# Starting every operand of TensorE at one SBUF byte address modulo 512

## The chip, the core and the metric

The kernel is one program on one core of a Trainium2 chip. The metric is device time of one execution in microseconds (us). Before the change the median of three runs is 1791.74 us (1791.64 to 1792.22). The core has five engines that matter here: TensorE (PE in the rows: matmuls, with PEld for the loads of the stationary operand), VectorE (DVE), ScalarE (ACT), GpSimd (POOL) and SyncE (SP, which issues most transfers). SBUF is the on-chip memory: 128 partitions, and every tile takes the same byte range in each of them. PSUM holds matmul results.

A matmul has two operands in SBUF. The *stationary* one (up to 128 columns) is loaded into the array first, which the rows show as LDWEIGHTS on PEld; the *moving* one (up to 512 columns) is then streamed through it. In a row `ps<-hx,wh 128*128 128x512` the moving tile is `hx`, the stationary one `wh`; 128*128 are rows and columns of the stationary operand, 128x512 is the result.

## The reference

Two layers of a diffusion transformer over 256 tokens and 256 context tokens, width 2048, branch width 4096, all in float32. Cut to what matters:

```python
# layer 0 (x and ctx alike): h = rmsnorm(x) * (1 + scale) + shift
u, z = split(h @ w_in, 2)                                # 2048 -> 2 x 4096
f = real(fft2(u grouped in 16 x 256, over tokens and channels))
y = (f @ w_mix, group by group) * silu(z)                # 16 matrices 256 x 256
x = x + gate * (y @ w_out[0])                            # 4096 -> 2048
# layer 1 (x only; the context gives keys and values)
q, k, v, z = split(h @ w_in1)
o = attention(rope(q), rope(k), v, window 128, all context keys, a sink per head)
x = x + gate * ((o * silu(z)) @ w_out[1]);  return rmsnorm(x, final_g)
# scale, shift, gate = silu(c) @ ada_w + ada_b, once per layer and per stream
```

## The kernel before, in words

**Precision.** Each float32 operand is split into a high part in the fp32r type (ACT copies it, rounding) and a low part (DVE subtracts): names end in `h` and `l`. `mm3` (lines 78 to 81) multiplies with three fp32r matmuls: high by high (line 79), high by low (line 80), low by high (line 81). Nearly all of PE's work is such triples; lines 1142 and 1144 are a two-matmul form of the same, with results of 512 and 256 columns.

**Stages**, by time in the profile:

- 0 to 51 us: norms, the Fourier transform over tokens as a matmul (`xs` stationary, `dh`/`dl` moving, 256 columns) and transposes.
- 51 to 144 us, first z: six blocks of z for layer 0 (`ext` tiles moving, 512 columns, `wh`/`wl` stationary), mixed with float32 matmuls for scale and shift (line 320).
- 144 to 378 us, **u stage**: 16 groups. For each, weights of u are loaded, folded into a difference `m` and a sum `p` of 127 columns for each of 16 row blocks (`load_uh`, `split_uh`), and split into `wmh`, `wml`, `wph`, `wpl`. `part` multiplies them as stationary operands with `hx` and `act` tiles moving: 256 columns for `m`, 260 for `p`. `load_m` prepares the mixing matrix of the group (`mh`/`ml` moving, tables `ch`/`cl` stationary), and `mix` multiplies that (`pqh`, `pql`, `sp` stationary) with the split results (`am`, `aph`/`apl`, `asp` moving).
- 378 to 670 us, rest of z: 26 blocks of 48 matmuls, weights `wh`/`wl` stationary, activations moving, 512 columns; of the 16 row blocks' activation tiles some lie in pool `hx`, some in pool `act` (`h_tile`).
- 670 to 1021 us, first output projection: 32 times 48 matmuls, 512 columns; moving are `hx` tiles.
- 1031 to 1116 us, keys and values of layer 1: moving are the weights `wh`/`wl`, stationary the activations `h1` (pool `h1`) and `h1c`.
- 1116 to 1640 us, q, z and attention, in an order written out by hand.
- 1640 to 1779 us, last projection: weights moving, stationary the split results `yh[k]` in 32 tiles from several pools; those for k from 28 on lie in the pool `fin` and are named `ys`, as are the 12 before them, which lie in `h1`.

**Where a tile lies** is set by the pools: a pool takes a range of bytes in each partition, a tile its offset in it, and sizes of the tiles that stand before it shift all that follow. Tiles of 2048 or 4096 bytes in a row keep the same address modulo 512; a small tile ahead of them moves them all.

**What sets the order of the work.** The framework's scheduler orders each engine's instructions by a timing model of its own, from the program's dependencies; only the attention part is written out (`tc.manual_schedule`). So a change of an instruction's shape can reorder the stages around it. Each engine then works through its list in order, with semaphore waits. A tile buffer that is used again makes the next writer wait for the last reader. Big weights come over SP's queue into `raw` (3 buffers of 8 KB per partition), split halves go into `ws` (6 buffers of 4 KB), the split weights of u into `wf` (8 of 4 KB).

The addresses of the operands, in bytes modulo 512, read from the built programs:

| operand tiles | where they are used | before | after |
|---|---|---|---|
| `wh`, `wl` in `ws`; `act`; `raw` | all over | 192 | 256 |
| `hx` | moving in u, rest of z, first projection | 256 | 256 |
| `ext` | moving in first z | 352 | 256 |
| `wmh`, `wml`, `wph`, `wpl`, row block k of 8 | stationary in u | 256 - 4k | 256 |
| `mh`, `ml` of `load_m` | moving | 480 | 256 |
| `ch`, `cl`; `pqh`, `pql`, `sp`; `asp` | u stage | 256 | 256 |
| `am` (named `mh`, `ml` too) | moving in `mix` | 288 | 256 |
| `aph`, `apl` (1040 bytes each) | moving in `mix` | 352, 384, 416, 448 | the same |
| `dh`, `dl`, `xs` | first stage | 256 | 256 |
| `h1`, `h1c`, `ye`, `ys` in `h1`, `kkh`, `kkl`, `qa`, `qb` | layer 1 | 192 | 256 |
| `ys` in `fin` (k from 28) | stationary, last projection | 256 | 256 |
| `raw2` (line 320, float32) | moving in first z | 448 | 448 |

Of the kernel before, what the change touches and what calls it, by code (L numbers as in the profile page):

```python
# [10 lines left out]
F32 = mybir.dt.float32  # L11
F32R = mybir.dt.float32r
# [4 lines left out]
P = 128  # L17
# [5 lines left out]
G = 16  # L23
# [6 lines left out]
def tile_dit(ctx: ExitStack, tc: tile.TileContext, a: dict, out: bass.AP):  # L30
# [24 lines left out]
    def cload(name, shape, q=None, pool=const):  # L55
        t = pool.tile(shape, F32, tag=name, name=name)
        (q or nc.gpsimd).dma_start(t, a[name])
        return t
# [73 lines left out]
    def wf(name, dt=F32):  # L132
        return wfp.tile([P, 1024], dt, tag="wf", name=name)

    def split_uh(v, m, nms=("m", "p")):
        fl = {}
        for nm, t in [(nm, {"m": m, "p": v}[nm]) for nm in nms]:
            l, h = (wf(f"w{nm}{x}", F32R)[:, : 8 * 127].rearrange("p (k c) -> p k c", k=8) for x in "lh")
            split(h, l, t)
            fl[nm] = (h, l)  # L140
        return fl
# [15 lines left out]
    adap = lay0.enter_context(tc.tile_pool(name="ada", bufs=1))  # L157
# [22 lines left out]
    with tc.tile_pool(name="st", reuse_waits="tile", bufs=1, side="right") as st, ExitStack() as sts:  # L180
        dm = sx.tile([P, 2, N], F32, name="dm")
        ss = st.tile([P, 4, 4], F32, name="ss")
        rr = st.tile([P, 4], F32, name="rr")
        f0 = st.tile([P, KT, 2], F32, name="f0")
        sh16 = st.tile([P, KT, 2], F32, name="sh16")

        cnt = [0]

# [298 lines left out]
        for i in range(4):  # L487
            for j in range(4):
                k = 4 * i + j
# [28 lines left out]
        for b in range(NE):  # L518
            z = ext()
# [1 line left out]
            nc.gpsimd.dma_start(zd[b], z)  # L521

    uc = us.enter_context(tc.tile_pool(name="uc", reuse_waits="tile", bufs=2, side="right"))
    mk = cload("mk", [96, G], pool=adap)
    wsr = wsp.tile([P, 512], F32, tag="ws", name="wsr")
    nc.gpsimd.dma_start(wsr, a["wsp"])
    sphl = []
# [7 lines left out]
    def load_m(g):  # L535
        m = uc.tile([P, 2, GD], F32, tag="m", name="m", bufs=1) if g else wsp.tile([P, 2, GD], F32, tag="ws", name="m")
        (nc.scalar if g else nc.gpsimd).dma_start(m, a["wm"][g])
        mt = wsp.tile([P, 2, GD], F32, tag="ws", name="mt")
        lr = uc.tile([P, 2, GD], F32R, tag="ml", name="ml")
        mh = uc.tile([P, 2, GD], F32R, tag="mh", name="mh")  # L540
        V.tensor_tensor(mt[:, 0], m[:, 0], m[:, 1], op=ALU.add)
        V.tensor_tensor(mt[:, 1], m[:, 0], m[:, 1], op=ALU.subtract)
        split(mh, lr, mt)
        o = psum()
        mm3(o[:, 0:GD], ch[:, 0, :], cl[:, 0, :], mh[:, 0, :], lr[:, 0, :], True, False)
        PE.matmul(o[:, 0:GD], ch[:, 2, :], mh[:, 1, :], start=False, stop=False)
        PE.matmul(o[:, 0:GD], ch[:, 2, :], lr[:, 1, :], start=False, stop=True)
        mm3(o[:, GD : 2 * GD], ch[:, 1, :], cl[:, 1, :], mh[:, 1, :], lr[:, 1, :], True, True)
        o2 = psum()
        PE.matmul(o2[0:96, 0:GD], ch[:, 3, 0:96], mh[:, 0, :], start=True, stop=False)  # L550
        PE.matmul(o2[0:96, 0:GD], ch[:, 3, 0:96], lr[:, 0, :], start=False, stop=True)
        pqh = ua.tile([P, 512], F32R, tag="pqh", name="pqh")
        pql = ua.tile([P, 512], F32R, tag="pql", name="pql")
        split(pqh, pql, o)
        sp = ua.tile([96, GD], F32R, tag="sp", name="sp")
        S.activation(sp, o2[0:96, 0:GD], AF.Copy, scale=mk[:, g : g + 1])
        V.scalar_tensor_tensor(sp[64:96, :], o2[64:96, 0:GD], mk[64:96, g : g + 1], sp[64:96, :].bitcast(F32), op0=ALU.mult, op1=ALU.subtract)
        return pqh, pql, sp
# [3 lines left out]
    fd = [dram.tile([P, 512], F32, name=f"fd{b}") for b in range(NB)]  # L562
    rawu = us.enter_context(tc.tile_pool(name="rawu", reuse_waits="tile", bufs=1))
    up = us.enter_context(tc.tile_pool(name="up", reuse_waits="tile", bufs=2))
    asp = up.tile([96, 2, 130], F32R, name="asp", bufs=1)
    for g in range(G):
        w = load_u(g) if g else wu0
        if g == 0:
            am = []
            for i in range(2):  # L570
                mh = up.tile([P, 2, P], F32R, name=f"mh{i}", bufs=1)
                ml = up.tile([P, 2, P], F32R, name=f"ml{i}", bufs=1)
                for z in (mh, ml):
                    for s in range(2):
                        S.activation(z[:, s], ident, AF.Copy, scale=0.0)
                am.append((mh, ml))
        if g:
            pqh, pql, sp = load_m(g)
        oa = {}

        def part(xs, ks=range(KT)):
            for nm, c0, c1 in xs:
                if nm not in oa:
                    oa[nm] = psum()[0:127, 0 : 2 * (c1 - c0)].rearrange("p (s j) -> p s j", s=2)
            for k in ks:
                for nm, c0, c1 in xs:
                    wh, wl = w[k // 8][nm]
                    h, l = hx[k]
                    mm3(oa[nm], wh[:, k % 8, :], wl[:, k % 8, :], h[:, :, c0:c1], l[:, :, c0:c1], k == 0, k == KT - 1)

        if g < G - 1:
            part(parts[:1])
        else:
            mix()
            part(parts)
        if g == 0:
            o2 = psum()[0:64, 0:260].rearrange("p (s j) -> p s j", s=2)
            for k in range(KT):
                for x_ in hx[k]:
                    sp_end = PE.matmul(o2, sphl[k // 8][:, k % 8], x_[:, :, 0:130], start=k == 0 and x_ is hx[k][0], stop=k == KT - 1 and x_ is hx[k][1]).ins  # L600
            osl = up.tile([32, 2, 130], F32, name="osl", bufs=1)
            S.copy(osl, o2[32:64])
            osp = up.tile([32, 2, 130], F32, name="osp", bufs=1)
            V.tensor_tensor(osp, o2[0:32], osl, op=ALU.add)
            S.copy(asp[0:32], osp)
            S.copy(asp[64:96], osp)
            V.tensor_tensor(asp[32:64], osp, asp[0:32].bitcast(F32), op=ALU.subtract)
            with tc.issue_after(sp_end):
                pqh, pql, sp = load_m(0)
        mh, ml = am[g % 2]  # L610
        split(mh[0:127, :, 1:128], ml[0:127, :, 1:128], oa["m"][:, :, 1:128])
        if g < G - 1:
            if g:
                mix()
            part(parts[1:])
        ph = up.tile([127, 2, 130], F32R, tag="aph", name="aph")
        pl = up.tile([127, 2, 130], F32R, tag="apl", name="apl")
        split(ph, pl, oa["p"])

        def mix(g=g, mh=mh, ml=ml, ph=ph, pl=pl, pqh=pqh, pql=pql, sp=sp):  # L620
            for db in range(2):
                q = slice(db * P, (db + 1) * P)
                q2 = slice(GD + db * P, GD + (db + 1) * P)
                gs_ = psum()
                gv = gs_[:, 0:256].rearrange("p (s j) -> p s j", s=2)
                mm3(gv, pqh[0:127, q2], pql[0:127, q2], mh[0:127], ml[0:127], True, True)
                gc = psum()
                gcv = gc[:, 0:260].rearrange("p (s j) -> p s j", s=2)
                PE.matmul(gcv, sp[:, q], asp, start=True, stop=False)  # L629
                mm3(gcv, pqh[0:127, q], pql[0:127, q], ph, pl, False, True)  # L630
                gsb = up.tile([P, 2, P], F32, tag="gsb", name="gsb")
                S.copy(gsb, gv)
                ft = up.tile([P, 2, N], F32, tag="ft", name="ft")
                V.tensor_tensor(ft[:, :, 0:128], gcv[:, :, 0:128], gsb, op=ALU.subtract)
                V.tensor_tensor(ft[:, :, 129:256], gcv[:, :, 1:128], gsb[:, :, 1:128], op=ALU.add)
                S.copy(ft[:, :, 128:129], gcv[:, :, 128:129])
                (nc.gpsimd if g < G - 1 else nc.scalar).dma_start(fd[g * 2 + db], ft.rearrange("p s j -> p (s j)"))

        if g == G - 1:
            mix()  # L640
# [38 lines left out]
    with tc.tile_pool(name="yp", reuse_waits="tile", bufs=32) as ypool:  # L679
# [19 lines left out]
        with tc.tile_pool(name="zp", reuse_waits="tile", bufs=2) as zp:  # L699
# [11 lines left out]
            for kg in range(4):  # L711
                wr = rawp.tile([P, D], F32, tag="raw", name="raw")
                last_dma[0] = nc.sync.dma_start(wr.rearrange("p (b c) -> p b c", b=4), a["wz"][NE - 4 : NE, :, kg * 512 : (kg + 1) * 512].rearrange("b p c -> p b c")).ins
                w = []
# [5 lines left out]
                for j in range(4):  # L720
                    k = kg * 4 + j
# [9 lines left out]
            for b in range(NE):  # L731
                z = zp.tile([P, 512], F32, tag="z", name="z")
# [3 lines left out]
            for b in range(NE + 4, NB):  # L736
                w = ws_split(raw(a["wz"][b - 4]))
# [43 lines left out]
        for i in range(32):  # L781
# [3 lines left out]
            w = ws_split(raw(a["wo0"][sw, kg]))  # L785
# [16 lines left out]
            edge = kg in (0, 15)  # L802
# [84 lines left out]
    with tc.tile_pool(name="h1", reuse_waits="tile", bufs=16) as h1p:  # L887
        hx1 = []
        kT = []
        with tc.tile_pool(name="kvp", reuse_waits="tile", bufs=2) as kvp:  # L890
# [18 lines left out]
            for kg in range(8):  # L909
                w = [(kv_h, kv_l)] if kg == 0 else ws_split(raw(a["wkv"][kg]))  # L910
                for j in range(2):
                    k = kg * 2 + j
# [4 lines left out]
                    for tb in range(4):  # L917
                        h = (hx1, hc1)[tb // 2][k]
                        c = (tb % 2) * P
# [27 lines left out]
        with tc.tile_pool(name="ye", reuse_waits="tile", bufs=6) as yep, ExitStack() as ats:  # L947
# [349 lines left out]
            with tc.tile_pool(name="fin", reuse_waits="tile", bufs=1) as fp:  # L1297
# [7 lines left out]
                        nc.gpsimd.dma_start(x2[tb][c], x1d[tb, :, c * 512 : (c + 1) * 512])  # L1305
                fg = fp.tile([P, D], F32, name="fg")
                nc.gpsimd.dma_start(fg, a["fg"].broadcast_to([P, D]))
                ss = fp.tile([P, 10], F32, name="ss")

                def evac(tb, cb, o):  # L1310
                    q, t, x = slice(cb * 512, (cb + 1) * 512), act(), x2[tb][cb]
# [20 lines left out]
                for k in range(28, NB, 2):  # L1332
                    w = w1_next()
# [5 lines left out]
                for kg in range(16):  # L1339
                    w = ws_split(raw(a["wo1b"][kg]))  # L1340
# [179 lines left out]
```

## Time and profile before

| what | value |
|---|---|
| median of three runs | 1791.74 us (1791.64 to 1792.22) |
| span of the profiled execution | 1790.8 us, 27995 instructions |
| what lies around the span, median less span | 0.9 us |
| PE busy | 1770.2 us (99%), 10941 matmuls |
| DVE, ACT, POOL busy | 1376.3 (77%), 880.1 (49%), 185.7 us (10%) |
| moved by DMA | 370.20 MB, mean 207 GB/s |
| granted TensorE clock | full in all 40 slices |

How to read it: the execution's own time is its span and what lies around it, and the page gives the span. A matmul's bar in the rows is longer than the distance to the next one's start, since matmuls are pipelined and their ends are modelled: bars of 0.39 us start every 0.23 us. What sets the time of a stream of matmuls is that distance, which this document calls the *pace*. It can be had from a window of W us that n bars touch: a bar touches it if it starts in the window or up to one bar's length ahead of it, so the pace is (W + bar) / n.

### The profile page before, as it was taken

To read this page: it belongs to the slowest core of one execution; us is meant where nothing else is said; L and a number is where in the kernel's file an instruction comes from. 1 tells how busy PE (TensorE), PEld (TensorE's weight loads), DVE (VectorE), ACT (ScalarE), POOL (GpSimd) and SP (SyncE) were. 2 spreads that over 40 slices of the span, in tenths; PEclk is the share of its full clock that TensorE was granted. 3 is DMA by queue.
4 is the path that set the end of the run, shared out by engine and by line. 5 is a ranking of instruction groups with operands and counts; after the bars stand their busy time and mean duration, and the time that the engine had idled before them with its cause. 6 is when DMAs were issued, how large, how long until landed. Compare 5 with 4: busy or idle time off the path is not lost.

```text
span 1790.8 us, 27995 instructions
## 1 busy us (share of the span) xinstructions
PE 1770.2 (99%) x10941; PEld 1482.2 (83%) x10941; DVE 1376.3 (77%) x2314; ACT 880.1 (49%) x1530; POOL 185.7 (10%) x225
## 2 busy tenths in 40 slices
PE   8999999999999999999999999999999999999997
PEld 6669999987888888888888888888888888887886
DVE  5769999978887887687986473797889888977454
ACT  6545444543222232233332352687678777866343
POOL 0001000020000010000000001133123303301010
PEclk9999999999999999999999999999999999999999
DMA  9994555476766677654566233544444344446553
GB/s 388 420 368 167 200 205 207 165 270 226 306 243 234 255 261 273 266 197 159 211 237 233 104 148 107 187 143 152 152 148 148 139 146 156 143 156 246 195 186 120
DMA packets 69028, 370.20 MB, mean 207 GB/s; under 512 B 8736, under 2 KB 10928, under 8 KB 35360
## 3 DMA queue, kind: packets, MB, share of 16 engines
q1 hardware_dynamic: 55344, 328.51, 49.0%
q0 software_dynamic: 9520, 32.96, 5.4%
q10 hardware_dynamic: 4032, 6.95, 1.1%
q8 instruction: 86, 1.41, 0.3%
q14 instruction: 46, 0.38, 0.1%
HBM read 353.16 MB, written 15.21 MB: 206 GB/s over the span
## 4 chain that ended last, share of the span: by engine, by line
PE 97%; DVE 1%; ACT 1%; issue 0%; DMA 0%; SPq 0%; DVEq 0%
PE ps L79 26%; PE ps L81 25%; PE ps L80 25%; PE ps L1142 7%; PE ps L1219 3%; PE ps L1144 3%; PE ps L320 2%; PE ps L1173 2%; PE ps L1174 2%; PE ps L1015 0%; DMA xn<-in_x 0%; PE ps L600 0%; PE ps L629 0%; PE ps L336 0%; DVE wl L1092 0%
## 5 line engine op out<-in xcount | busy, mean ns | idle before, releaser
L69 ACT CAST wh<-raw 128x1024 fp32r<-128x1024 f32 x178 | 186.8, 1052 | 415.5 <-PE ps L80 369.8
L70 DVE TENSOR_TENSOR wl<-raw,wh 128x1024 fp32r<-128x1024 f32 x178 | 219.9, 1236 | 145.8 <-ACT wh L69 145.3
L79 PE MATMUL ps<-hx,wh 128*128 128x512 f32 x700 | 274.5, 395 | 0.0
L81 PE MATMUL ps<-hx,wl 128*128 128x512 f32 x700 | 273.2, 393 | 0.0
L80 PE MATMUL ps<-hx,wh 128*128 128x512 f32 x700 | 273.0, 390 | 0.0
L1092 DVE TENSOR_TENSOR wl<-raw,wh 128x1024 fp32r<-128x1024 f32 x142 | 190.5, 1347 | 56.6 <-ACT wh L1086 55.8
L1086 ACT CAST wh<-raw 128x1024 fp32r<-128x1024 f32 x142 | 148.8, 1048 | 76.3 <-PE ps L80 55.2
L1142 PE MATMUL ps<-h,wh 128*128 128x512 f32 x512 | 184.3, 399 | 0.0
L666 DVE CUSTOM_DVE_ANT_0 raw<-raw,cb 128x1024 f32<-128x1024 f32 x128 | 154.9, 1220 | 31.8 <-DMA raw<-in_adw 31.1
L81 PEld LDWEIGHTS ps<-hx,wl 128*128 128x128 f32 x700 | 131.4, 188 | 31.0
L80 PEld LDWEIGHTS ps<-hx,wh 128*128 128x128 f32 x700 | 131.4, 188 | 29.6
L79 PEld LDWEIGHTS ps<-hx,wh 128*128 128x128 f32 x700 | 131.5, 188 | 27.8 <-ACT hx L405 0.8
L1144 PE MATMUL ps<-h,wl 128*128 128x256 f32 x512 | 138.6, 281 | 0.0
L666 DVE CUSTOM_DVE_ANT_0 junk<-raw,cb 128x1024 f32<-128x1024 f32 x96 | 117.2, 1221 | 24.8 <-DMA raw<-in_adw 15.0
L79 PE MATMUL ps<-wh,h 128*128 128x512 f32 x320 | 124.8, 396 | 0.2 <-ACT h L899 0.2
L80 PE MATMUL ps<-wl,h 128*128 128x512 f32 x320 | 124.5, 389 | 0.0
L81 PE MATMUL ps<-wh,h 128*128 128x512 f32 x320 | 124.4, 390 | 0.0
L1142 PEld LDWEIGHTS ps<-h,wh 128*128 128x128 f32 x512 | 96.3, 188 | 21.5
L1191 ACT ACTIVATE p<-ps,mx 128x512 f32<-128x512 f32 x128 | 86.8, 683 | 53.4 <-DVE mx L1182 52.9
L1144 PEld LDWEIGHTS ps<-h,wl 128*128 128x128 f32 x512 | 96.6, 189 | 2.9
L81 PE MATMUL ps<-act,wl 128*128 128x512 f32 x234 | 91.0, 394 | 0.7 <-DVE wl L70 0.7
L1182 DVE CUSTOM_DVE_ANT_0 ps<-ps,mask,nsink 128x512 f32<-128x512 f32 x128 | 91.1, 752 | 0.5
(367 smaller groups left out, 4012.8 us busy)
## 6 DMA issues: line engine op xcount, KB each, us to landing
raw<-in_adw SPq DMA_DIRECT2D x64, 1024.0 KB, 4.9
raw<-in_wz SPq DMA_DIRECT2D x58, 1024.0 KB, 4.8
raw<-in_awp SPq DMA_DIRECT2D x32, 1024.0 KB, 12.0
raw<-in_wo SPq DMA_DIRECT2D x32, 1024.0 KB, 4.9
raw<-in_wq SPq DMA_DIRECT2D x32, 1024.0 KB, 4.8
raw<-in_wu SPq DMA_DIRECT2D x25, 1016.0 KB, 5.1
raw<-in_wo1b SPq DMA_DIRECT2D x16, 1024.0 KB, 4.8
act<-in_xT POOLq DMA_DIRECT2D x32, 256.0 KB, 5.6
```

The source lines that it names most:

```text
L69: cast[0] = S.copy(h, t[:, i * 1024 : (i + 1) * 1024]).ins
L70: V.tensor_tensor(l, t[:, i * 1024 : (i + 1) * 1024], h.bitcast(F32), op=ALU.subtract)
L79: PE.matmul(o, wh, xh, start=start, stop=False)
L80: PE.matmul(o, wh, xl, start=False, stop=False)
L81: return PE.matmul(o, wl, xh, start=False, stop=stop).ins
L666: V.tensor_tensor_reduce(junk if s == 0 and i < 3 else wf, wf, cb[:, s], 1.0, 0.0, ALU.mult, ALU.add, acc[:, i, kh, fg * 2 + f, s : s + 1])
L1086: cast[0] = S.copy(h, t[:, i * 1024 : (i + 1) * 1024]).ins
L1092: V.tensor_tensor(ready[n][1], ready[n][2], ready[n][0].bitcast(F32), op=ALU.subtract)
L1142: PE.matmul(o[0], wh[:, q], hx1[k], start=k == 0, stop=k == KT - 1)
L1144: PE.matmul(o[0][:, 0:N], wl[:, q], hx1[k][:, 0:N], start=False, stop=False)
L1182: V.tensor_tensor_reduce(so[tb], so[tb], mask[:, tb, :], -0.125, nsink[:, i : i + 1], ALU.add, ALU.min, mx[:, tb : tb + 1])
L1191: S.activation(pt[:, tb, :], so[tb], AF.Exp, bias=mx[:, tb : tb + 1], scale=-1.0, accum_out=sm[:, tb : tb + 1])
```

## The change

Five edits, all of them on addresses:

- The split weights of u are held at 128 columns for each row block (512 bytes) where they were at 127 (508 bytes); the 127 columns that are used stay the same. The copies and subtractions that write them get the shape 128x8x127 where they had 128x1016.
- Padding tiles: 24 columns `edge` in pool `st`, ahead of `raw3` and `ext` in the right-hand stack; 56 columns `edge` in pool `uc`; the tile `ss` of the last stage grows from 10 to 128 columns.
- The table `mk` (96x16) moves from pool `ada` to pool `const`, which moves `raw`, `ws`, `act` and the pools of layer 1 by 64 bytes.
- The four zero-padded tiles `am` are allocated ahead of `asp`. What is computed, and with how many instructions, stays the same.

```diff
@@ split_uh
-            l, h = (wf(f"w{nm}{x}", F32R)[:, : 8 * 127].rearrange("p (k c) -> p k c", k=8) for x in "lh")
+            l, h = (wf(f"w{nm}{x}", F32R).rearrange("p (k c) -> p k c", k=8)[:, :, 0:127] for x in "lh")
@@ pool st
         sh16 = st.tile([P, KT, 2], F32, name="sh16")
+        st.tile([P, 24], F32, name="edge")
@@ after the first z
-    mk = cload("mk", [96, G], pool=adap)
+    mk = cload("mk", [96, G])
@@ load_m
         mh = uc.tile([P, 2, GD], F32R, tag="mh", name="mh")
+        if g == 1:
+            uc.tile([P, 56], F32, name="edge", bufs=1)
@@ u stage
+    am = [tuple(up.tile([P, 2, P], F32R, name=f"m{x}{i}", bufs=1) for x in "hl") for i in range(2)]
     asp = up.tile([96, 2, 130], F32R, name="asp", bufs=1)
...
-            am = []
-            for i in range(2):
-                mh = up.tile([P, 2, P], F32R, name=f"mh{i}", bufs=1)
-                ml = up.tile([P, 2, P], F32R, name=f"ml{i}", bufs=1)
-                for z in (mh, ml):
+            for pair in am:
+                for z in pair:
                     for s in range(2):
                         S.activation(z[:, s], ident, AF.Copy, scale=0.0)
-                am.append((mh, ml))
@@ last stage
-                ss = fp.tile([P, 10], F32, name="ss")
+                ss = fp.tile([P, P], F32, name="ss")
```

The scheduler answers the new shape with another order in the u stage, and there alone but for one pair swapped on DVE, ACT and PE in the last stage. Lists of SP and POOL are as before. Two places matter to the prediction.

The first is PE in the third group of the u stage: `wph`/`wpl` and `wmh`/`wml` are products with the weights of u, `apl,pqh` and `aph,pql` the second half of `mix` for the group before. Before:

```order
L79 MATMUL ps<-act,wph 127x260
L80 MATMUL ps<-act,wph 127x260
L80 MATMUL ps<-apl,pqh 128x260
L81 MATMUL ps<-aph,pql 128x260
L80 MATMUL ps<-apl,pqh 128x260
L81 MATMUL ps<-aph,pql 128x260
L81 MATMUL ps<-act,wpl 127x260
L79 MATMUL ps<-hx,wph 127x260
```

With the change:

```order
L79 MATMUL ps<-hx,wph 127x260
L80 MATMUL ps<-apl,pqh 128x260
L81 MATMUL ps<-aph,pql 128x260
L80 MATMUL ps<-apl,pqh 128x260
L81 MATMUL ps<-aph,pql 128x260
L80 MATMUL ps<-hx,wph 127x260
L81 MATMUL ps<-hx,wpl 127x260
```

The four products of `mix` stand 16 places into the group's `p` products, where they stood 8 places in.

The second is DVE at the start of the u stage, where the first weights of u and the first mixing matrices are split (`wpl`, `wml`: low parts of the weights; `wm`: a new difference; `ml`, `mt`: the mixing matrix; line 694: activations for the next stage). Before:

```order
L62 TENSOR_TENSOR wml<-wm,wmh 128x1016
L694 SCALAR_TENSOR_TENSOR act<-act,gs_83,r_bc 128x256 x2
L62 TENSOR_TENSOR ml<-mt,mh 128x512
L541 TENSOR_TENSOR mt<-m 128x256
L542 TENSOR_TENSOR mt<-m 128x256
L128 TENSOR_TENSOR wm<-raw 128x1016
L62 TENSOR_TENSOR wpl<-raw,wph 128x1016
L62 TENSOR_TENSOR ml_1643<-ps,mh_1642 127x2x127
L604 TENSOR_TENSOR osp<-ps,osl 32x260
```

With the change:

```order
L62 TENSOR_TENSOR wml<-wm,wmh 128x8x127
L62 TENSOR_TENSOR ml<-mt,mh 128x512
L62 TENSOR_TENSOR wpl<-raw,wph 128x8x127
L62 TENSOR_TENSOR ml_1643<-ps,mh_1642 127x2x127
L694 SCALAR_TENSOR_TENSOR act<-act,gs_83,r_bc 128x256
L604 TENSOR_TENSOR osp<-ps,osl 32x260
L694 SCALAR_TENSOR_TENSOR act<-act,gs_83,r_bc 128x256
L544 TENSOR_TENSOR mt<-m 128x256
L545 TENSOR_TENSOR mt<-m 128x256
L128 TENSOR_TENSOR wm<-raw 128x1016
```

The low part `wpl` of the first group comes ahead of the next group's difference `wm` and mixing matrix `mt`, where it came behind them (lines from 184 on have moved by one to three).

## The prediction

> **What bounds the kernel now.** I read the engines' shares and the chain of work that ended last first, then PE's waits, since a change of addresses can only matter where PE itself sets the time.
>
> ```profile
> PE 1770.2 (99%) x10941; PEld 1482.2 (83%) x10941; DVE 1376.3 (77%) x2314; ACT 880.1 (49%) x1530; POOL 185.7 (10%) x225
> ...
> PE 97%; DVE 1%; ACT 1%; issue 0%; DMA 0%; SPq 0%; DVEq 0%
> ```
>
> ```profile
> PE ps L294 <- DMA xn<-in_x: 5.8, 1, 5.8
> PE ps L79 <- ACT dh L259: 1.7, 1, 1.7
> PE ps L81 <- DVE wl L70: 0.7, 1, 0.7
> PE ps L861 <- ACT act L822: 0.4, 1, 0.4
> PE ps L79 <- ACT h L899: 0.2, 1, 0.2
> ```
>
> PE is 97% of the chain and waits 8.8 us in all, 7.5 of them before its first real stage. So the time is the number of matmuls times their pace, and the question is whether the pace depends on addresses. Windows inside stages that run matmuls of 512 columns only answer it (us, busy and count, clock, DMA share, GB/s):
>
> ```profile
> 440.00:660.00 220.00, 220.00 (x950) 1.00 0.68 256
> 680.00:1010.00 330.00, 330.00 (x1444) 1.00 0.57 213
> 1034.00:1112.00 78.00, 78.00 (x346) 1.00 0.29 109
> 1666.00:1724.00 58.00, 58.00 (x258) 1.00 0.54 196
> ```
>
> With 0.39 us for a bar, the paces are 220.39/950 = 232.0 ns in the rest of z, 330.39/1444 = 228.8 in the first projection, 78.39/346 = 226.6 for keys and values and 58.39/258 = 226.3 in the last projection. PE is busy for every microsecond and the clock is full in all four, so the difference is no wait and no throttle. It is the same mm3 at the same shapes. By the table of addresses the last two windows have both operands at 192 modulo 512. The first projection has the moving one at 256 and the stationary one at 192; the rest of z has the moving one alternately at 192 and 256 over weights at 192.
>
> The cleanest comparison lies inside the last projection, one line and one loop, where only the pool of the stationary tile changes: `fin` tiles at 256, everything else at 192.
>
> ```profile
> 1724.12 0.39 PE L81 MATMUL ps<-wh,act 128*128 128x512 f32 x1
> 1724.34 1.10 PE L79 MATMUL ps<-wh,ys 128*128 128x512 f32 x4
> ...
> 1735.54 0.62 PE L79 MATMUL ps<-wh,ye 128*128 128x512 f32 x2
> ```
>
> ```profile
> 1720.00:1745.00 25.00, 11.36 (x48) 1.00 0.51 184
> ```
>
> The second fence counts the matmuls with `ys` alone: 48 from 1724.34 to 1735.54, which is 233.3 ns each, against 226.3 on either side. A different residue of the two operands costs 2 to 7 ns of 227. I take 226.6 as the pace at equal residues.
>
> **Term 1: 512 columns in z and the projections.** No instruction is added or removed; SP's and POOL's lists stay as they are. After the change all these operands start at 256.
>
> - Rest of z: 26 blocks of 48, 1248 matmuls. At the window's pace, 232.0 less 226.6 on all of them gives 6.7 us. The stretch ahead of it is partly flat (first four blocks, which run a moving tile four times in a row):
>
> ```profile
> 380.00:440.00 60.00, 59.31 (x263) 48.22 (x262) 46.59 (x87) 25.28 (x43) 3.23 (x6) 1.00 0.63 226
> ```
>
> 59.70/263 is 227.0 ns (its 0.7 us of idle time taken out), so 985 by 5.4 ns and 263 by 0.4, 5.4 us, is the lower bound. I take the middle: 6.1 us.
> - First projection: 32 times 48, 1536 matmuls, by 228.8 - 226.6 = 2.2 ns: 3.4 us.
> - First z, `ext` at 352, 270 matmuls. Their bars, beside one at equal residues:
>
> ```profile
> L79 PE MATMUL ps<-ext,wh 128*128 128x512 f32 x90 | 36.3, 415 | 0.0
> L81 PE MATMUL ps<-ext,wl 128*128 128x512 f32 x90 | 35.7, 396 | 0.0
> L80 PE MATMUL ps<-ext,wh 128*128 128x512 f32 x90 | 35.5, 394 | 0.0
> L80 PE MATMUL ps<-wl,h1c 128*128 128x512 f32 x64 | 24.6, 389 | 0.0
> ```
>
> A bar is 389 where the pace is 226.6, so it exceeds the pace by 162. Lines 80 and 81 are then at 232 to 234; line 79 has the restarts after float32 matmuls in it, which stay. 270 by 6 ns: 1.6 us. DMA is busy in this stage, but PE has no wait on it above.
> - Last projection: `fin` tiles, 48 + 24 + 12 matmuls of 512 columns by 7 ns: 0.6 us.
>
> Sum of term 1: 11.7 us. Nothing behind PE takes it back: in those stages PE gains at most 2.3%, and of the rest DVE is the nearest, busy 193.5 of 230 us in the rest of z:
>
> ```profile
> 145.00:375.00 230.00, 229.91 (x1910) 229.70 (x1909) 213.89 (x306) 111.72 (x219) 20.11 (x38) 1.00 0.57 200
> 430.00:660.00 230.00, 229.44 (x989) 185.85 (x990) 193.50 (x289) 60.89 (x68) 1.07 (x2) 1.00 0.69 260
> ```
>
> (The columns are PE, PEld, DVE, ACT, POOL.) If that cover were gone, the 6.1 us would be lost with it.
>
> **Term 2: the u stage.** Here 256 and 260 columns stream while a weight of 127 columns loads, and aligned rows of that exact kind don't exist. Before:
>
> ```profile
> L79 PE MATMUL ps<-act,wph 128*127 128x260 f32 x144 | 41.1, 285 | 0.0
> L79 PE MATMUL ps<-hx,wph 128*127 128x260 f32 x112 | 31.9, 285 | 0.0
> L80 PE MATMUL ps<-act,wmh 128*127 128x256 f32 x144 | 40.4, 281 | 0.0
> L80 PE MATMUL ps<-ml,ch 128*128 128x256 f32 x32 | 9.0, 280 | 0.0
> ```
>
> Less 162, the pace is 123 for the 768 `p` products and 118 to 119 for the 768 `m` products and for `load_m`. The nearest aligned rows are the first stage's, 256 columns and all at 256:
>
> ```profile
> 48.53 0.28 PE L80 MATMUL ps<-dl,xs 128*128 128x256 f32 x1
> ...
> 49.49 0.28 PE L79 MATMUL ps<-dh,xs 128*128 128x256 f32 x1
> ```
>
> Nine starts there (eight steps) take 0.96 us: 120 ns, flat, and above the 118.5 of the misaligned ones. Equal residues thus make a short matmul steadier and not faster. I take 120 for `m` (+1.2 us) and for the 160 of `load_m` (+0.3). For 260 columns I add four columns at the slope between 256 and 512, (226.6 - 120)/256 = 0.42 ns, which gives 121.7: -1.0 us on 768. Sum +0.5 us. Bounds: the two misaligned columns show 118 to 123, so `p` could fall to 120 and `m` stay (-2.3 us). On the dear side stands the one aligned stream that isn't flat, lines 1142 and 1144, everything at 192:
>
> ```profile
> 1165.82 0.40 PE L1142 MATMUL ps<-h,wh 128*128 128x512 f32 x1
> ...
> 1170.41 0.40 PE L1142 MATMUL ps<-h,wh 128*128 128x512 f32 x1
> ```
>
> Thirteen pairs in 4.59 us: 353 ns, where 226.6 + 120 would be 347. Equal residues don't suffice when lengths alternate; 3 ns per matmul of that kind on 1536 is another 4.6 us, so term 2 lies between -2.3 and +5.
>
> `aph` and `apl` keep their odd addresses, and lines 1142, 1144, 1173, 1174 and 1219 had equal relations before and keep them: 0 each.
>
> **Term 3: the new order and the new shape.** A strided 128x8x127 operand exists already (line 129) beside a contiguous one (line 62):
>
> ```profile
> L62 DVE TENSOR_TENSOR wml<-wm,wmh 128x1016 fp32r<-128x1016 f32 x31 | 37.4, 1208 | 0.0
> L129 DVE TENSOR_TENSOR raw<-raw 128x1016 f32<-128x1016 f32 x23 | 27.8, 1211 | 0.2
> ```
>
> 1208 against 1211: 0. The order in the u stage moves the second half of `mix` later on PE, behind 16 products instead of 8, which gives its producers about 1 us more. On DVE it puts `wpl` of the first group ahead of `wm` of the next: the first is safer, the second later by some 1.2 us. PE's list of waits above has next to nothing for that stage; DVE is busy 213.9 of 230 us in it, so 16 us of slack cover it. I take 0, with 0 to +2.5 us (two DVE instructions) as bounds; if DVE's cover went, each of them would cost 1.2 us.
>
> **The sum.** -11.7 + 0.5 + 0 = -11.2 us on a span of 1790.8, hence 1779.6, and with the 0.9 us between span and median **1780.5 us**, 0.6% less.
>
> **The rivals.**
>
> *No effect of addresses.* The paces would then belong to the stages (which operand is weights, which pool) and stay: 1791.7 us. For it: lines 1142 and 1144 are not flat at equal residues. Against it: the 48 matmuls above, which differ from their neighbours in nothing but the stationary tile's pool.
> The Trainium skill, page "TensorE: Matmul & The Clock Gate", Part 2, step 1 of "Step-by-step", speaks for this rival: weight loads and the moving operand have separate SBUF read ports, and "Loading the next tile's weights doesn't steal SBUF read bandwidth from the running matmul." By that rule no pair of addresses could slow a stream, and the time would stay at 1791.7. The trace disagrees by 7 ns in 226 on those 48 matmuls, so I give it little.
>
> *The u stage takes much of it back.* At +5 us, or with +2.5 us of waits on top of +2, the sum is -6.7 to -7.2, so 1784.5 to 1785. For it: the aligned 120 above the misaligned 118.5, and DVE at 93% in that stage. Against it: within a part all lengths are the same, unlike lines 1142 and 1144.
>
> *Slower: equal residues are the collision.* Moving reads and weight reads that start at one residue would meet in the same place, and long runs with one constant shape would merely fall into step. Then the rest of z, where moving tiles change with each row block, stays at 232.0, and the projection at 228.8; the u stage goes to 120 and 126 (121.7 and the 3 ns above, and 1 more since the 260 columns are two runs of 130): 768 x 1.5 + 768 x 3 + 160 x 1.5 = 3.7 us. That is 1795.4. It decides if `p` costs over 125 and the long matmuls gain nothing. For it: 120 over 118.5. Against it: keys and values change the moving tile with nearly every matmul too (high part, low part, two halves of 512), with all of them at one residue, and run at 226.6.
>
> **How the numbers follow.** About 0.2% (3.6 us) is what a measurement of this kernel can tell from no change. The forecast holds 0.72, its own range 1778 to 1783 from term 2 between -2.3 and +2.5; the u stage that takes much back 0.16; no effect 0.08; slower 0.04. Up to 1788.2 counts as faster: 0.88. Same 0.08, slower 0.04. The range for 8 in 10 goes from 1777.5 to 1786.5, through the second case.
>
> **What would show it.** In the changed profile, windows of the rest of z and of the first projection at 226.6 ns with bars of 389 on lines 79, 80 and 81 alike; the `fin` tiles no slower than their neighbours; the u stage 234 us long within 3, with its bars at 282 and 284. Wrong would be: 232 again in the rest of z (addresses don't matter), or PE waits on DVE of over 2 us in the u stage.

## The result and the profile after

| | before | after | difference |
|---|---|---|---|
| median | 1791.69 us (1791.15 to 1792.22, 4 runs) | 1781.01 us (1780.30 to 1782.29, 4 runs) | -10.7 us |
| ratio | | 0.9941, interval 0.9930 to 0.9953 | |
| span of the profiled execution | 1790.8 us | 1779.3 us | -11.5 us |

The kernel is 0.6% faster; the forecast was 1780.5 us. On the page of the profile after, the engines' shares and the chain of work that ended last:

```profile
PE 1757.8 (99%) x10941; PEld 1480.4 (83%) x10941; DVE 1375.5 (77%) x2314; ACT 880.7 (49%) x1530; POOL 185.3 (10%) x225
...
PE 97%; DVE 1%; ACT 1%; DMA 1%; issue 0%; SPq 0%; DVEq 0%; ACTq 0%
```

The same 10941 matmuls are still 97% of the chain. PE is busy for 12.4 us less, and DVE, ACT and POOL are within 0.8 us of before: it is PE's work that became shorter, not its waits. The waits of PE after:

```profile
PE ps L295 <- DMA xn<-in_x: 5.5, 1, 5.5
PE ps L79 <- ACT dh L260: 2.2, 1, 2.2
PE ps L79 <- ACT h L899: 1.0, 1, 1.0
PE ps L81 <- DVE wl L70: 0.8, 1, 0.8
PE ps L861 <- ACT act L822: 0.4, 1, 0.4
```

They sum to 9.9 us where they were 8.8. So the gain is in the pace. Windows of the rest of z, of the first projection and of keys and values, after (us, busy and count, clock, DMA share, GB/s):

```profile
440.00:650.00 210.00, 210.00 (x928) 1.00 0.69 262
680.00:1000.00 320.00, 320.00 (x1413) 1.00 0.58 215
1025.00:1100.00 75.00, 75.00 (x332) 1.00 0.30 108
```

By (W + 0.39)/n the paces are 226.7, 226.7 and 227.1 ns, where before had 232.0, 228.8 and 226.6 (one bar more or less in a window moves these figures by 0.2 to 0.7). All three stages now have one pace. The groups of instructions say the same in bars (busy us, mean ns):

```profile
L80 PE MATMUL ps<-hx,wh 128*128 128x512 f32 x700 | 272.3, 389 | 0.0
L79 PE MATMUL ps<-hx,wh 128*128 128x512 f32 x700 | 270.8, 389 | 0.0
L81 PE MATMUL ps<-hx,wl 128*128 128x512 f32 x700 | 270.7, 389 | 0.0
L79 PE MATMUL ps<-ext,wh 128*128 128x512 f32 x90 | 36.0, 411 | 0.0
L80 PE MATMUL ps<-ext,wh 128*128 128x512 f32 x90 | 35.3, 393 | 0.0
L81 PE MATMUL ps<-ext,wl 128*128 128x512 f32 x90 | 35.2, 391 | 0.0
L80 PE MATMUL ps<-act,wmh 128*127 128x256 f32 x144 | 40.9, 284 | 0.0
L79 PE MATMUL ps<-act,wph 128*127 128x260 f32 x144 | 40.8, 284 | 0.0
```

The 2100 matmuls with `hx` moving are at 389 on all three lines. The `ext` tiles went from 415, 394 and 396 to 411, 393 and 391: less than to 389. In the u stage the 256-column product of line 80 rose from 281 to 284, where the prediction had 282, and the 260-column one of line 79 fell from 285 to 284.

The last projection, at its `fin` tiles (named `ys`), which ran at 233.3 ns before. The whole lies 11 us earlier here:

```profile
1713.17 0.39 PE L81 MATMUL ps<-wh,act 128*128 128x512 f32 x1
1713.39 1.07 PE L79 MATMUL ps<-wh,ys 128*128 128x512 f32 x4
...
1724.05 0.39 PE L81 MATMUL ps<-wh,ys 128*128 128x512 f32 x1
1724.27 0.62 PE L79 MATMUL ps<-wh,ye 128*128 128x512 f32 x2
```

```profile
1709.00:1734.00 25.00, 11.04 (x48) 1.00 0.52 190
```

The second fence counts the matmuls with `ys` alone, as in the prediction: 48 of them start between 1713.39 and 1724.27, which is 226.7 ns each, no slower than their neighbours.

By the start of the first matmul of each stage in the two traces, in us (keys and values from their first product with `h1c`; the last `mix` is counted with the rest of z):

| stage | before | after | difference | forecast |
|---|---|---|---|---|
| transform | 45.5 | 44.1 | -1.4 | 0 |
| first z | 92.5 | 91.5 | -1.0 | -1.6 |
| u stage | 233.9 | 234.4 | +0.5 | +0.5 |
| rest of z | 291.9 | 285.8 | -6.0 | -6.1 |
| first projection | 351.6 | 348.2 | -3.4 | -3.4 |
| up to keys and values | 10.1 | 11.0 | +0.8 | 0 |
| keys, values | 84.7 | 84.7 | 0.0 | 0 |
| q, z, attention | 523.7 | 523.7 | 0.0 | 0 |
| last projection | 139.9 | 139.3 | -0.6 | -0.6 |

These are -11.1 us; the rest of the span's 11.5 lies ahead of the first matmul (-0.3) and in rounding.

### The profile page after: what moved, and what is told of

It reads as the page before. It is cut to its first block, busy times and chain, and to the rows that moved or that the text cites. A ratio compares the mean times of both kernels' runs of the same rounds, so it can differ in the third digit from the quotient of the medians.

```text
span 1779.3 us, 27989 instructions
## 1 busy us (share of the span) xinstructions
PE 1757.8 (99%) x10941; PEld 1480.4 (83%) x10941; DVE 1375.5 (77%) x2314; ACT 880.7 (49%) x1530; POOL 185.3 (10%) x225
## 4 chain that ended last, share of the span: by engine, by line
PE 97%; DVE 1%; ACT 1%; DMA 1%; issue 0%; SPq 0%; DVEq 0%; ACTq 0%
PE ps L79 26%; PE ps L81 25%; PE ps L80 25%; PE ps L1142 7%; PE ps L1219 4%; PE ps L1144 3%; PE ps L321 2%; PE ps L1173 2%; PE ps L1174 2%; PE ps L1015 0%; DMA xn<-in_x 0%; DMA x1d<-act 0%; PE ps L629 0%; PE ps L600 0%; PE ps L337 0%
```

## The experiments

Theory: a stream of 512-column matmuls runs at its flat pace when its moving and its stationary operands begin at one residue, and the move of `mk`, which brings the weights to the `hx` tiles, is the part that pays. Rivals: the padding or the pitch does it; the addresses have no part in it (a new order); equal residues modulo 512 are not what counts.

**The table alone.** Before, with one line of the change:

```diff
-    mk = cload("mk", [96, G], pool=adap)
+    mk = cload("mk", [96, G])
```

> The kernel before with the table mk moved alone: act, ws, raw and the pools of layer 1 go from 192 to 256 modulo 512; ext stays at 352, the u weights at a pitch of 508 bytes, mh/ml at 480, the order on every engine is the one of before. Theory (the relation of moving tile and weight modulo 512 sets the pace): the rest of z and the first projection become flat at 226.7 ns, which are 6.1 and 3.4 us; first z keeps its 92.5 us; the fin tiles come to lie at 320 against 256 and stay slow; the u stage stays at 234 us; about 1782.2 us. Rival (the gain of the whole change came from the new order of the u stage or from the padding): 1791.7 us, both windows as before.

Measured: 1780.65 us (1780.07 to 1782.34), ratio 0.9939, interval 0.9922 to 0.9955. The order of every engine is that of before. The same two windows:

```profile
440.00:650.00 210.00, 210.00 (x929) 1.00 0.69 260
680.00:1000.00 320.00, 320.00 (x1414) 1.00 0.58 214
```

The rest of z is 285.8 us and the first projection 348.2, as after the whole change. A table of 64 bytes per partition that is kept somewhere else, and nothing more, gives all of the gain. The rival "no effect of addresses" falls with this run: instructions, shapes and order are those of before. The u stage is even shorter here, 232.7 us: its 256-column matmuls stay at 118.2 ns and its 260-column ones go from 122.7 to 121.8. In the two profiles the other four edits give 0.9 us in the first z and 0.6 in the last projection and take 1.7 in the u stage. Of these 1.7 us some is the execution: the run with grouped lengths below has the same u stage as this one, in order and addresses, and took 234.0 us for it, with one wait of 1.0 us that this one does not have.

**The pitch alone.** Before, with the weights of u at 128 columns:

```diff
-            l, h = (wf(f"w{nm}{x}", F32R)[:, : 8 * 127].rearrange("p (k c) -> p k c", k=8) for x in "lh")
+            l, h = (wf(f"w{nm}{x}", F32R).rearrange("p (k c) -> p k c", k=8)[:, :, 0:127] for x in "lh")
```

> The kernel before with the 128-column pitch of the u weights alone: stationary tiles of u all at 256, moving hx at 256, moving act at 192; nothing else moves. Theory: the long matmuls keep 232.0 and 228.8 ns, the u stage changes by -1 to +1.5 us, 1791 to 1793 us. Rival (the pitch is worth something by itself, since weights that start on odd addresses load slower): the u stage shorter by 3 us or more, 1788.5 us or less.

Measured: 1791.82 us (1791.36 to 1793.68, 10 runs), ratio 0.9996, interval 0.9986 to 1.0006: no change.

```profile
440.00:650.00 210.00, 210.00 (x908) 1.00 0.70 260
680.00:1000.00 320.00, 320.00 (x1400) 1.00 0.59 217
```

Nothing moves in the long stages (231.7 and 228.9 ns by the starts). The u stage is 234.8 us: 118.9 ns for 256 columns and 121.8 for 260, and one wait of 1.2 us that before does not have:

```profile
PE ps L80 <- DVE apl L62: 1.2, 1, 1.2
```

This run also corrects the section on the change, which puts the new order in the u stage down to the new shape 128x8x127. With the new shape alone the order is that of before on every engine; the 24 columns `edge` in pool `st` alone bring the order that the two places of that section show.

**A distance put back, in four sizes.** The changed kernel, with a pad ahead of `hx`. With `hx` move the tiles of the first stage, the split weights of u, the tables and the operands of `mix`, and the weights of 144 of the 270 products with `ext` in the first z. In the rest of z and the first projection it is `hx` alone that moves away from its weights:

```diff
+    adap.tile([P, 32], F32, name="shift")
```

Of 32 columns, 128 bytes:

> The changed kernel with a pad of 128 bytes ahead of the hx tiles, so that hx is at 384 and act, ws stay at 256 (the first stage and the u weights move along with hx). Theory: the first projection, all hx moving over ws weights, goes back to 228.8 ns or more (by 2 to 7 ns: 3.4 to 10 us longer), the rest of z to 231 or more (5 to 8 us longer); 1789 to 1799 us. Rival (what counts is that tiles start on a round address, and 384 is a multiple of 128): both stay at 226.7 ns, 1781 us.

Of 64 columns, 256 bytes:

> The same with 256 bytes, hx at 0 modulo 512 against 256. If the relation counts modulo 512: first projection 229 to 233 ns and rest of z 231 to 233, 1789 to 1799 us. If it counts modulo 256 or less: both flat at 226.7 ns, 1781 us.

Of 8 columns, 32 bytes:

> The changed kernel with hx 32 bytes on, the smallest step that tiles can take: 288 against 256. If any difference modulo 256 costs: first projection above 227 ns, at 227.5 to 229 (64 bytes gave 228.9, 128 gave 233.3). If a difference has to reach 64 bytes to count: flat at 226.7 ns.

Of 48 columns, 192 bytes:

> The changed kernel with hx 192 bytes on, 448 against 256, which is -64 modulo 256. The fin tiles lay at that difference with the roles exchanged (moving 64 below the stationary tile) and took 233.3 ns; if the sign matters, so does this one: 233 ns in the first projection, 10 us longer, 1798 us. If only the distance counts: 228.9 ns as at 64, 3.4 us, with the rest of z 1788 to 1791 us.

Measured, one run each (with the changed kernel and before beside them; paces by the starts, in ns):

| `hx` stands above the weights by | time, us | first projection | rest of z |
|---|---|---|---|
| 0 (after) | 1781.01 | 226.67 | 226.75 |
| 32 bytes | 1798.12 | 233.33 | 231.26 |
| 64 bytes (before) | 1791.69 | 228.89 | 231.67 |
| 128 bytes | 1798.99 | 233.33 | 231.15 |
| 192 bytes | 1798.69 | 233.33 | 231.41 |
| 256 bytes | 1781.31 | 226.67 | 226.73 |

The window 680 to 1000, which lies inside the first projection in all of them, for 128, 256, 32 and 192 bytes, a fence each:

```profile
680.00:1000.00 320.00, 320.00 (x1373) 1.00 0.57 214
```

```profile
680.00:1000.00 320.00, 320.00 (x1413) 1.00 0.58 215
```

```profile
680.00:1000.00 320.00, 320.00 (x1373) 1.00 0.58 214
```

```profile
680.00:1000.00 320.00, 320.00 (x1373) 1.00 0.58 214
```

1373 bars are 233.3 ns, 1413 are 226.7. The clock is full in all of them and PE is never idle, so it is not a throttle and not a wait. With 128 bytes the bars of one line go from 389 to 395:

```profile
L79 PE MATMUL ps<-hx,wh 128*128 128x512 f32 x700 | 274.5, 395 | 0.0
```

Three things follow. First, the address decides, in both directions: the same instructions, in the same order on every engine, run 17 to 18 us slower with a pad of 32 to 192 bytes. Second, 256 bytes are as good as 0, so on these distances the relation counts modulo 256; the 512 of the title is stricter than what these runs need. Third, the loss does not grow with the distance. 32 bytes already cost 6.7 ns of 226.7, as much as 128; the expectation of 227.5 to 229 for that step was wrong. Of the distances tried only 64 bytes lies between the ends, and 192, which is 64 the other way round, does not. The `fin` tiles of before agree with that: there the moving operand stood 64 bytes below the stationary one, and they ran at 233.3.

The row of 64 bytes comes from another kernel, with its weights at 192 instead of 256. The first z of the same runs supplies it once more at other addresses, in a row of 72 or more products with `ext` whose weights moved with `hx`. With the pad of 192 bytes `ext` stands 192 bytes below these weights, which is 64 above modulo 256, and they run at 228.9 ns by the starts. At a distance of 256 they run at 226.7, at 32 below at 233.3 and at 128 below at 232.4; in before, where `ext` stood 96 bytes above the same weights, at 233.3. So it is the distance that counts, modulo 256 and with its sign.

**The table, the `fin` tiles and the pad of `ext`.** The changed kernel without the pitch, the pad in `uc` and the move of `am`:

> The kernel before with the table moved, ss at 128 columns and the 24 columns in pool st (ext at 256); u weights at 508 bytes, mh/ml at 480, am where it was. Building it shows that the pad in st is what changes the order in the u stage. Theory: first z 91.5 us instead of 92.4, last stage 139.3 instead of 139.9, u stage 233 to 234 us with the new order (m at 118, p at 122 ns, 1 us of waits): 1779.5 us. Rival (the pitch of the u weights is what pays for the new order): u stage at 234.5 or above, 1781 us.

Measured: 1781.25 us, one run; span 1779.5. The first z is 91.5 us and the last projection 139.3, as expected, but the u stage is 235.2, 2.5 more than with the table alone and past the 233 to 234 that were expected; its paces of 118.2 and 121.9 ns are within 0.1 of the table's. What is added is waits, of which the list shows the longest:

```profile
PE ps L79 <- ACT mh L61: 1.6, 1, 1.6
```

This kernel has the order that the pad in `st` brings, the same on every engine as the changed kernel's. The figures are the rival's, but not its reason: the changed kernel with a pad of 256 bytes has the pitch and this order too, and its u stage took 235.6 us, with a wait of 0.8 on the same line. All four pads show that wait, 0.8 to 1.5 us; the changed kernel's own profile does not. In single profiles, then, the pad in `st` gains 0.9 us in the first z and its order costs 1.7 to 2.9 us in the u stage against the table's 232.7, or less against the 234.0 of the grouped kernel. That it pays is not shown: with it the kernels took 1781.01 and 1781.25 us, without it 1780.65.

**The lengths grouped.** Before with the table moved, `ss` grown, and the two-matmul form of layer 1's z (lines 1142 and 1144) in another order, the 512-column matmuls of a unit first and its 256-column ones then:

```diff
-                    for k in range(i * 8, i * 8 + 8):
+                    ks = range(i * 8, i * 8 + 8)
+                    last = [(KT - 1, 0)] if i else []
+                    for k, part in [(k, 0) for k in ks if k < KT - 1] + [(k, 1) for k in ks] + last:
...
-                        for part in (0, 1) if k < KT - 1 else (1, 0):
```

> The kernel before with the table moved, ss at 128 columns (fin tiles at 256 like the rest), and the z units of layer 1 written with their matmuls of 512 columns in a row and those of 256 columns in a row, where they alternated (lines 1142 and 1144 of the kernel before); order elsewhere as before. Theory (at equal residues the pace is flat when the length is constant, and alternating lengths break it): the 353 ns of a pair become 226.7 + 120 = 346.7, 3.4 us on 512 pairs, the fin tiles give 0.6: 1780.65 - 4.0 = 1776.6 us. Rival (the pair is dear since its short matmul cannot cover the load of the weight behind it, whatever the order): a pair stays at 353 ns, 1780 us.

Measured: 1778.02 us (1777.24 to 1779.08), ratio to before 0.9924, interval 0.9910 to 0.9937: the fastest of the kernels here, 3.0 us below the changed one by the medians. The attention stage goes from 491.4 to 488.0 us. First the changed kernel, then this one (start, bar, count at the end; in this kernel the two lines are 1143 and 1145):

```profile
1155.44 0.40 PE L1142 MATMUL ps<-h,wh 128*128 128x512 f32 x1
1155.68 0.28 PE L1144 MATMUL ps<-h,wl 128*128 128x256 f32 x1
...
1159.68 0.40 PE L1142 MATMUL ps<-h,wh 128*128 128x512 f32 x1
```

```profile
1161.00 1.98 PE L1143 MATMUL ps<-h,wh 128*128 128x512 f32 x8
1162.81 1.12 PE L1145 MATMUL ps<-h,wl 128*128 128x256 f32 x8
1163.77 1.78 PE L1143 MATMUL ps<-h,wh 128*128 128x512 f32 x7
1165.38 1.12 PE L1145 MATMUL ps<-h,wl 128*128 128x256 f32 x8
1166.33 0.40 PE L1143 MATMUL ps<-h,wh 128*128 128x512 f32 x1
1166.57 0.40 PE L1174 MATMUL ps<-kkh,qb 128*128 128x512 f32 x1
```

Alternating, twelve pairs take 4.24 us: 353 ns a pair. Grouped, eight of 512 columns take 1.81 us (226 each) and eight of 256 take 0.96 (120 each): 346 a pair. The next seven of 512 columns take 1.61 (230), right behind a change of length. Over the stage a pair costs 349.1 by the starts, so some two thirds of the 6.6 ns come back. The rival, that a pair costs 353 in any order, falls. What is left is lost behind each change of length.

The 3.4 us of the stage are as many as were expected of the pairs, but by luck: 512 pairs at 4.2 ns give 2.1 us. The matmuls of 512 columns behind them (lines 1173 and 1174 of the kernel before) lose some 0.5, and another 1.7 come from the products of line 1219, which the grouping does not touch (changed kernel, then grouped):

```profile
L1219 PE MATMUL ps<-pall,vr 32*64 32x256 f32 x2048 | 63.5, 378 | 0.0
```

```profile
L1220 PE MATMUL ps<-pall,vr 32*64 32x256 f32 x2048 | 61.8, 377 | 0.0
```

By the starts they save it in every second group of 128, in the first products of the group (4.03 us a group, before 4.2 to 4.3). Why the order of the pairs does that is not shown.

## Why the prediction was right

**The bound.** Right: PE sets the time, and its pace depends on addresses. The table's run and the four pads show it both ways.

**Term 1.** Rest of z -6.0 (forecast -6.1), first projection -3.4 (-3.4), last projection -0.6 (-0.6): the pace of 226.6 at equal residues is what was reached. In the rest of z the figure was right and its reason incomplete. The prediction let all 1248 matmuls gain, though the 702 with `act` moving had equal residues already and it gave no cost for taking turns. Nine row blocks at 226.67 and seven at 228.89 would be 227.6 on average; before ran at 231.67. So about four of the five nanoseconds that the change gains there come from ending the turns between two distances, and one from the distance itself. The first z gave 1.0 of 1.6. The step that was too large is "270 by 6 ns": it took the pace of all of them to 226.6, while it came to 229.8 (from 233.4). This stage mixes long fp32r matmuls with float32 ones, and the pace does not recover at once behind an interruption. Before already showed this behind its `fin` tiles, from 1735.54 on, where the operands are at one residue again:

```profile
1735.31 0.39 PE L81 MATMUL ps<-wh,ys 128*128 128x512 f32 x1
1735.54 0.62 PE L79 MATMUL ps<-wh,ye 128*128 128x512 f32 x2
1736.00 0.40 PE L80 MATMUL ps<-wl,ye 128*128 128x512 f32 x1
...
1736.93 0.39 PE L79 MATMUL ps<-wh,ye 128*128 128x512 f32 x1
...
1737.84 0.39 PE L80 MATMUL ps<-wl,ye 128*128 128x512 f32 x1
```

The first six behind the boundary take 1.39 us, 232 ns each; the next four take 0.91, 227 or 228 each. That is a run-in of about six matmuls. The rest of z of before agrees: in the 23 places where 12 or more aligned matmuls follow shifted ones, the first six take 232.1 ns on average, and from the ninth on 226.8. Where the two take turns every three matmuls, the aligned ones never get there: 232.6 ns beside the 233.0 of the shifted ones. The runs with a pad fit as well: the stage's 231.2 to 231.4 is above the mean by shares, nine row blocks at 226.7 and seven at 233.3, which is 229.6.

**Term 2.** Right in both parts, and in sum within 0.4 us. By the starts, all the 256-column matmuls of the stage went from 118.3 to 119.6 ns (forecast 120 for `m` and `load_m`) and the 260-column ones from 122.7 to 121.4 (forecast 121.7). On some 1018 and 912 of them that is +1.3 and -1.2 us, and waits add 0.4. The stage's +0.5 thus equals the forecast partly by chance: the paces give 0.1 of it. So the odd reading of before, that an aligned 256-column matmul is slower than a misaligned one, was no accident: with the table alone these matmuls stay misaligned, at 118.2. Aligning the short ones was a small loss, 1.4 ns each.

**Term 3.** The price, 0, was near in the one profile of the changed kernel: the u stage's waits rose by 0.4 us. That is partly luck. In all five other executions of this order (four pads, and the table with the pads of `ext` and `fin`) PE waits 0.8 to 1.6 us for ACT's split of `mh`, which stays within the bounds of 0 to 2.5; in this one it does not wait there. The order of before has such a wait too, 1.0 to 1.2 us for `apl`, in two of four executions. The reason given for the new order was wrong, since the new shape brings none.

**What was not forecast.** The transform is 1.4 us shorter. No edit touches it, and it takes 43.3 to 43.8 us in all eight experiments, the pitch alone included (43.6), where nothing of that stage moves. The profile of before is the odd one: for a few microseconds of this stage its granted clock was not full, which the page's row of slices of 45 us hides. From 14 to 18 us, before and after:

```profile
14.00:18.00 4.00, 3.98 (x21) 0.57 1.01 428
```

```profile
14.00:18.00 4.00, 4.00 (x34) 1.00 1.01 426
```

At 0.57 of the clock 4 us do the work of 2.3, so about 1.7 us were lost there (an estimate from this row). The nine other traces have the full clock there, the pitch alone included, so this is that one execution and not the change. Why the clock fell is not shown. That profile also makes before look longer than it is. In every run on record 1.7 to 1.8 us lie around the span; the 0.9 of the section on before and of the prediction is the median less the span of an execution that was some 0.8 us longer than the median one. The two cancel in the forecast, since its sum goes back to the median. The 0.8 us ahead of keys and values are the wait on line 899, 1.0 us in this execution where before had 0.2 and the table alone has 0.2. Without these two stages the table gives -10.5 us; the medians give -10.7, the forecast's terms -11.2.

**The rivals.** *No effect of addresses* fell. Each of the pads of 32, 128 and 192 bytes costs 6.7 ns of 226.7 on each matmul of the first projection. The Trainium skill, page "TensorE: Matmul & The Clock Gate", Part 2, step 1, says that loading the next weights takes no read bandwidth from the running matmul. Read as a rule on the time, by which these pads would cost nothing, it does not hold here. *The u stage takes much back* was worth 4.0 to 4.5 us; the stage took 0.5 more than before, and what the other edits took there beside the table is 1.7 in these two profiles. *Equal residues are the collision* fell in the rest of z, at 226.75. The sentence that equal residues do not suffice when lengths alternate was right, and it pointed to the version that is faster still.

**Open.** Which of the two reads gives way, and why: not shown. In the prediction's rows the matmul just ahead of the first `fin` tile starts at 1724.12 and the next at 1724.34, so it is not slow, although the weight after it already stands at another residue. A collision of a matmul with the next load, one by one, is thus too simple a story. That 64 bytes cost less than 32, 128 and 192 is measured, in two stages, and not explained. A pitch for the 260-column products alone, which by the paces would give 0.4 us, was not tried.

## What to carry to other kernels

Where PE is busy without gaps at a full clock and two stages of the same shape run at different paces, compare the addresses of their operands: a tile of 64 bytes in the wrong pool cost 0.6% here. Bring the moving and the stationary operands of long streams to one address modulo 256 with the smallest move that does it, then see whether each further pad changes the scheduler's order, and leave short matmuls as they are. A stream that takes turns between two distances every few matmuls loses on the aligned ones too. Keep runs of one length together: 512 and 256 columns in turn cost 353 ns a pair, in eights 349.

## What the runs showed of the hardware that was not expected

- The distance of the two operands counts modulo 256 bytes and with its sign: a pad of 256 gives 226.67 ns as 0 does, and 192 below gives 228.9 as 64 above does.
- The loss is a step: 32, 128 and 192 bytes all give 233.33 ns for 512 columns in the first projection, and only 64 lies between (228.89).
- Aligned streams run at exactly repeating paces: 226.67 for 512 columns and 120 for 256, which is 0.417 ns for a column and 13.3 ns for each matmul, if the two are put on one line.
- 256 columns are faster misaligned (118.2 to 118.3) than aligned (119.6 to 120).
- After a change of residue the pace takes some six matmuls to come back (232 ns, then 227); turns of three aligned and three shifted matmuls run at 232.6 and 233.0.
